# Reading the moving operand backwards in four projections, and shifting the weight tiles in steps of 64 bytes

## The chip, the cores and the metric

The kernel runs on one core of a Trainium2 chip. The metric is the device time of one execution in microseconds (us), the median of several runs; lower is better.

## What is computed

One layer of an autoregressive decoder on 256 tokens of width 2048, float32, and a final norm:

```python
h = rms_norm(x, ln1)
proj = h @ w_in                       # 2048 -> GDN q|k|v, beta, decay, z; MoBA q|k|v; gates a, b
qkv_a, beta_a, decay_a, z_a, qkv_b, gate_a, gate_b = split_columns(proj)
y_a = gated_deltanet(qkv_a, beta_a, decay_a, z_a, ...) @ w_branch_a      # 1024 -> 2048
y_b = moba_attention(rope(q_b), rope(k_b), v_b) @ w_branch_b             # 1024 -> 2048
merged = sigmoid(gate_a) * y_a + sigmoid(gate_b) * y_b
x = x + merged @ w_out                                                   # 2048 -> 2048
h = rms_norm(x, ln2)
u = causal_dwconv(h @ w_up, ffn_conv, ffn_conv_bias)                     # 2048 -> 2 x 5632
u_gate, u_val = split(u, 2)
x = x + (silu(u_gate) * u_val) @ w_down                                  # 5632 -> 2048
return rms_norm(x, final_norm)
```

## The kernel before

Activations lie transposed: 128 features of a block on the partitions, the 256 tokens along the free dimension. Every float32 operand of a projection is split into two parts that TensorE takes in one pass each, a high part (`wh`, `hh`) and the rest (`wl`, `hl`), and a product is the sum high x high + high x rest + rest x high. The two parts of an activation tile lie side by side (`hc`, `yc`, `mc`, `h2` are [128, blocks, 2, 256]), so that one matmul with `wh` as the stationary operand moves 512 columns (both parts of the activation) and one with `wl` moves 256 (the high part alone).

The stages follow each other: the GDN projections (PSUM tiles `ps_gdn`, `ps_z`), those of the attention (`ps_moba`, `ps_v`), the gates (`ps_gate`, 16 chunks), the two branch projections (`ps_br`, 8 times two chunks), the output projection (`ps_wo`, 8 chunks), the up projection (`ps_up`, 44 chunks) and the down projection (`pd`, 44 blocks of the hidden width, 24 matmuls each). Up to the fourth gate chunk the PSUM tiles are narrow and every matmul moves 256 columns; from then on they are wide. The GDN recurrence and the attention run as generators in the background, a step at a time between matmuls (`tick`, every 1700 units of matmul work).

`chunk` makes one PSUM tile from two weight tiles of 128 x 2048. `load_w` brings a weight tile by a DMA on SP's queue (`wraw`, four buffers), ACT copies it into `wh` (L118) and DVE subtracts to get `wl` (L115), both in pieces of 1024 columns; `wh` and `wl` have two buffers each. In `ps_v` and in the down projection the roles are exchanged: 512 columns of `wh` or `wl` move and 128 columns of an activation (`hc`; `ah`, `al`) are the weights. TensorE loads the weights of a matmul while the one before runs. In the compiled program the operand of each weight load begins at the last of its columns and steps by -1; the moving operand steps by +1.

All matmuls of `chunk` come from `main_mm` (L108), those of the down projection from `mmg` (L96). `yca` and `ycb` (L715) are the split branch outputs, `mc` the split merged branches, `h2` the split input of the up projection (L205, L206). In the recurrence, `X` (L514) is a copy of a unit matrix that is worked on in place and stored through a DRAM tile `dU` (L525) to be loaded as `U` (L527), and `Xa` (L512) comes through a DRAM tile `dA`. Which instruction stands where on an engine is set by a scheduler at build time; tile pools decide when a buffer can be written again.

Of the kernel before, what the change touches and what calls it, by code (L numbers as in the profile page):

```python
# [11 lines left out]
F32 = mybir.dt.float32  # L12
F32R = mybir.dt.float32r
# [6 lines left out]
P = 128  # L20
T = 256
D = 2048
KD = D // P
H = 8
KB = H
DFF = 5632
NF = DFF // P
EPS = 1e-6
EVERY = 1700
WIDE_AT = 4  # L30
ATT_SCALE = 128 ** -0.5
# [49 lines left out]
def layer_kernel(ctx: ExitStack, tc: tile.TileContext, xT, pos, cst, csel, ceye, vec, convw, ffw, bdv,  # L81
# [6 lines left out]
    wpool = wst.enter_context(tc.tile_pool(name="wpool", bufs=2))  # L88
# [4 lines left out]
    def mmg(ps, pairs, start=True, stop=True, **kw):  # L93
        n = len(pairs)
        for i, (a, b) in enumerate(pairs):
            pe.matmul(ps, a, b, start=(start and i == 0), stop=(stop and i == n - 1), **kw)  # L96
# [10 lines left out]
    def main_mm(ps, a, b, start, stop):  # L107
        pe.matmul(ps, a, b, start=start, stop=stop, skip_group_check=True)  # L108
        spent[0] += 215 if b.free_size() > T else 108
        if spent[0] >= EVERY:  # L110
            spent[0] = 0
# [5 lines left out]
    def split(hi, lo, src):  # L117
        act.copy(hi, src)  # L118
        return low(hi, lo, src)

    def three(ah, al, bh, bl):
        return [(ah, bh), (ah, bl), (al, bh)]
# [5 lines left out]
        sp.dma_start(raw[:, :n], src)  # L128
        return raw

    def load_w(src, n=2048, into=None, piece=1024, raw=None):
        raw = raw or fetch(src, n)
        wh, wl = into or [wpool.tile([P, 2048], F32R, name=t, tag=t) for t in ("wh", "wl")]
        for o in range(0, n, piece):
            lows.append(split(wh[:, o:o + piece], wl[:, o:o + piece], raw[:, o:o + piece]))
        return wh[:, :n], wl[:, :n]
# [8 lines left out]
    epst = keep.tile([P, 1], F32, name="epst")  # L145
    act.activation(epst, ones[:, 0:1], AF.Identity, scale=EPS)

# [26 lines left out]
            main_mm(ps, wh[:, k, :], x[:, k], k == 0, False)  # L174
            main_mm(ps[:, 0, :], wl[:, k, :], x[:, k, 0, :], False, k == kt - 1)

    def chunk(blocks, x, kt, name, raws=(None, None), piece=1024, steps=((0, 0, None), (1, 0, None))):
        ps = mmt("ps_" + name)
        ws = {}
        for j, k0, k1 in steps:  # L180
            if j not in ws:
                ws[j] = load_w(blocks[j], kt * P, raw=raws[j], piece=piece)
            block(ps[:, j], ws[j], x, kt, k0, k1)
        return ps

# [6 lines left out]
    def join(dst, ps, r):  # L192
        with tc.high_priority():
            join_(dst, ps, r)
# [26 lines left out]
    hp = hst.enter_context(tc.tile_pool(name="hp", bufs=1, side="right"))  # L221
    hc = hp.tile([P, KD, 2, T], F32R, name="hc", tag="hc")
# [4 lines left out]
    g = n1.enter_context(tc.tile_pool(name="n1", bufs=1, side="right"))  # L227
# [16 lines left out]
    for i in range(4):  # L244
        s = slice(4 * i, 4 * i + 4)
# [9 lines left out]
    raws = [fetch(w) for w in (w_gdn[2], w_gdn[3])]  # L255
# [38 lines left out]
    s = sdt("ps_bd")[:48, :T]  # L294
    mmg(s, [(wb2[:, k, :], x_[:, k, :]) for k in range(KD) for x_ in (hh, hl)])
    R1 = rstd([sq[0][:, 0, :], sq[0][:, 1, :]], fk, "R1")
    R1b = both(R1)
# [21 lines left out]
    m = m_st.enter_context(tc.tile_pool(name="m", bufs=2, reuse_waits="tile"))  # L319
    gdn_st = ExitStack()  # L320
    dr = gdn_st.enter_context(tc.tile_pool(name="dr", bufs=2, space=bass.MemoryType.DRAM))
    g = gdn_st.enter_context(tc.tile_pool(name="g", bufs=2, side="right", reuse_waits="tile"))
# [118 lines left out]
    def gdn(h0, kq, v):  # L441
# [9 lines left out]
        st = g.tile([P, 8, 4], F32, name="st")  # L451
        dve.tensor_scalar(st[:, 0, :], pq[:, :, 0], EPS, P * EPS, op0=ALU.add, op1=ALU.mult)

# [4 lines left out]
        for j in range(2):  # L458
            c = 8 + hs[j]
# [25 lines left out]
        act.activation(st[:, 2, :], st[:, 1, :], AF.Sqrt, bias=epst)  # L485
        dve.tensor_scalar(st[:, 3, :], st[:, 1, :], EPS, None, op0=ALU.add)
        dve.reciprocal(st[:, 3, :], st[:, 3, :])
# [20 lines left out]
        dA = dr.tile([4, P + 1, P], F32, name="dA")  # L508
        pool.dma_start(dA[0:2, :P].rearrange("j s c -> s j c"), aq0[:, :, 0, :P])
        pool.dma_start(dA[2:4, :P].rearrange("j s c -> s j c"), aq1[:, :, 0, :])  # L510
        Xa = g.tile([32, 16, 16], F32, name="Xa")
        pool.dma_start(Xa, diag(dA))  # L512
        X = g.tile([32, 16, 16], F32, name="X")
        pool.tensor_copy(X, eye)  # L514
        yield from wait(9)
        for i in range(1, 16):
            tm = g.tile([32, 16, 16], F32, name="tm", bufs=1)
            dve.tensor_tensor(tm[:, :i, :i], X[:, :i, :i], Xa[:, None, :i, i].to_broadcast([32, i, i]), op=ALU.mult)
            dve.tensor_reduce(X[:, :i, i], tm[:, :i, :i], axis=AX.X, op=ALU.add, negate=True)
            if i % 4 == 3:  # L520
                yield
        dU = dUs[h0 // 2 % 2]
        if h0 < 4:
            sp.dma_start(dU[:, :P].rearrange("p s c -> s p c"), zero[:, None, :].to_broadcast([P, 4, P]))
        pool.dma_start(diag(dU), X)  # L525
        U = g.tile([P, 4, P], F32, name="U0", tag="U", bufs=1)
# [54 lines left out]
        pool.tensor_tensor(so, ot, ot, op=ALU.mult)  # L581
        dve.tensor_reduce(st[:, 4, :], so, axis=AX.X, op=ALU.add)
        dve.scalar_tensor_tensor(st[:, 5, :], st[:, 4, :], 1.0 / P, st[:, 0, :], op0=ALU.mult, op1=ALU.add)
# [11 lines left out]
    def pair(w, i):  # L595
        return [w[2 * i], w[2 * i + 1]]

    for gr in range(4):
# [3 lines left out]
        for a, t in enumerate((kq[:, 1], kq[:, 0], v)):  # L602
            if gr == 0 and a < 2:
                ps = (ps_q0, ps_k0)[a]
            else:
                ps = chunk(pair(w_gdn, 4 * gr + a), hc, KD, "gdn")
# [58 lines left out]
    for gr in range(4):  # L665
        h0 = 2 * gr
        qk = []
        for a in range(2):
            ps = chunk(pair(w_moba, 2 * gr + a), hc, KD, "moba")
            t = m.tile([P, 2, T], F32, name=f"qk{a}")  # L670
            join(t, ps, R1b)
            qk.append(t)
        if gr % 2 == 0:
            ps = [mmt("ps_v").rearrange("p a b -> p (a b)") for _ in range(2)]
            for q_ in range(4):
                wh, wl = (r3(t, 512) for t in load_w(w_mv[2 * gr + q_]))
                for i in range(2):
                    s = slice(i * P, (i + 1) * P)
# [18 lines left out]
    gts = gp.tile([P, 16, 2, T], F32, name="gts")  # L697
    for c in range(16):
        if c == WIDE_AT:
            while bg:  # L700
                tick()
            wide[0] = True
            psum_pools(3, 2)
        join(gts[:, c], chunk(pair(w_gate, c), hc, KD, "gate"), R1b)
        act.activation(gts[:, c], gts[:, c], AF.Sigmoid)
    while bg:
        tick()
# [1 line left out]
    yp = y_st.enter_context(tc.tile_pool(name="yp", bufs=1, side="right", reuse_waits="tile"))  # L709
    yc = []  # L710
    for t, nm_ in ((ya, "a"), (yb, "b")):
        yc.append(yp.tile([P, H, 2, T], F32R, name="yc" + nm_))
        for i in range(4):
            s = slice(2 * i, 2 * i + 2)
            act.copy(yc[-1][:, s, 0, :], t[:, s])  # L715
            low(yc[-1][:, s, 0, :], yc[-1][:, s, 1, :], t[:, s], pool)
# [1 line left out]

    m_st = ExitStack()
    m = m_st.enter_context(tc.tile_pool(name="mp", bufs=1, reuse_waits="tile"))  # L720
    mc = m.tile([P, KD, 2, T], F32R, name="mc")
    for c in range(8):
        bts = [yp.tile([P, 2, T], F32, name="bt", bufs=3) for _ in range(2)]
        join(bts[0], chunk(pair(w_ba, c), yc[0], H, "br"), gts[:, c])
        ps = chunk(pair(w_bb, c), yc[1], H, "br")
# [15 lines left out]
    b = bp.enter_context(tc.tile_pool(name="b", bufs=2, reuse_waits="tile"))  # L741
    x1 = bkeep.tile([P, KD, T], F32, name="x1")
    sqa = b.tile([P, 2, T], F32, name="sqa", bufs=1)
    h2 = hp.tile([P, KD, 2, T], F32R, name="h2", tag="hc")
    for c in range(8):
        steps = ((0, 0, KD - 2), (1, 0, 8), (0, KD - 2, KD), (1, 8, KD))
        ps = chunk(pair(w_o, c), mc, KD, "wo", **({} if c else dict(piece=512, steps=steps)))
        if c % 2 == 0:
            s = slice(2 * c, 2 * c + 4)
# [18 lines left out]
    ak = bk.enter_context(tc.tile_pool(name="ak", bufs=1, side="right", reuse_waits="tile"))  # L768
    acts = ak.tile([P, NF, T], F32, name="acts")
    for c in range(NF):  # L770
        ps = chunk([w_up[c], w_up[NF + c]], h2, KD, "up")
        un = b.tile([P, 2, T], F32, name="unf")
        join(un, ps, R2b)
        t = b.tile([P, 2, T], F32, name="cvf")
        for j in range(2):
            w = ffv[:, j * NF + c, :]
            act.activation(t[:, j, :], un[:, j, :], AF.Identity, scale=w[:, 2:3], bias=w[:, 3:4])  # L777
            for d in (1, 2):
                dve.scalar_tensor_tensor(t[:, j, d:], un[:, j, :T - d], w[:, 2 - d:3 - d], t[:, j, d:],  # L779
                                         op0=ALU.mult, op1=ALU.add)  # L780
        sg = b.tile([P, T], F32, name="sg")
        act.activation(sg, t[:, 0, :], AF.Silu)  # L782
        pool.tensor_tensor(acts[:, c, :], sg, t[:, 1, :], op=ALU.mult)  # L783
# [8 lines left out]
    pd = [[ps_d.tile([P, 512], F32, name=f"pd{i}_{n}") for n in range(4)] for i in range(2)]  # L792
# [8 lines left out]
    wl = {}  # L801
    tail = hp.tile([P, 2, 2, 2048], F32R, name="tail", tag="hc")

    def down(i, n, k, stop=False):
        ah, al, wh, wl_ = wl[k]
        s, c = slice(i * P, (i + 1) * P), slice(n * 512, (n + 1) * 512)
        mmg(pd[i][n], three(ah[:, s], al[:, s], wh[:, c], wl_[:, c]), start=False, stop=stop,
            skip_group_check=True)

    for k in range(NF):  # L810
        last = k >= NF - LAST
        ab = LAST if last else 2
        ah = b.tile([P, T], F32R, name="ah", tag="ah" + "L" * last, bufs=ab)
        al = b.tile([P, T], F32R, name="al", tag="al" + "L" * last, bufs=ab)
        split(ah, al, acts[:, k, :])
        wh, wl_ = load_w(w_dn[k], into=[tail[:, t, k - NF + 2, :] for t in range(2)] if k >= NF - 2 else None)
        wl[k] = (ah, al, wh, wl_)
        if not last:
            for i, n in order:
                if k == 0:  # L820
                    residual(i, n)
                down(i, n, k)
# [88 lines left out]
```

## Time and profile before

| | |
|---|---|
| time, median of 3 runs | 1512.03 us (1511.71 to 1512.86) |
| span of the profiled execution, first to last instruction | 1506.8 us |
| what lies around the span, against the median | 5.2 us |
| TensorE matmul busy | 1489.5 us (99%) |
| weight loads busy | 1337.8 us (89%) |
| VectorE / ScalarE / GpSimd busy | 1021.3 / 753.5 / 169.7 us |
| granted TensorE clock, mean | 0.998 |

The profiled execution's own time beside its span is not recorded apart from the runs, so the median stands for it. Busy time of TensorE counts the time in which at least one matmul is in flight; matmuls overlap, so their pace is read from the starts. In the rows, a group is named by what it writes and what it reads (`ps_up<-h,wh`), with its line, engine and shape.

### The profile page before, as it was taken

The page shows a single profiled execution, that of the slowest core. Times are in us where ns is not written, and L with a number is a line of the kernel's source. Part 1 is how long each engine was busy: PE and PEld are TensorE (multiplying, and loading weights), DVE is VectorE, ACT ScalarE, POOL GpSimd, SP SyncE. Part 2 cuts the span into 40 slices and gives each one's busy share as a digit, 9 for nine tenths or more (in the row PEclk, how much of TensorE's full clock was granted, in tenths as well). Part 3 has the DMA queues.
Part 4 walks back from the last instruction along what each step waited for, and adds up shares of the span by engine and source line. Part 5 has one row for each costly group of instructions (what it writes and reads, how often), then busy time and mean ns, then how long its engine had stood idle before and what let it go on. Part 6 is the DMA issues. An engine that isn't in the chain of part 4 may idle for free.

```text
span 1506.8 us, 22467 instructions
## 1 busy us (share of the span) xinstructions
PE 1489.5 (99%) x9167; PEld 1337.8 (89%) x9167; DVE 1021.3 (68%) x1454; ACT 753.5 (50%) x1021; POOL 169.7 (11%) x133
## 2 busy tenths in 40 slices
PE   9999999999999999999999999999999999999997
PEld 8999999988998888888888888888888888888886
DVE  7988695886765555777667767677676776555554
ACT  5655463434474444454455555455554554444444
POOL 1001101042130000110101211211112110000000
PEclk9999999999999999999999999999999999999999
DMA  9444444444335553567555555555555555555552
GB/s 340 174 169 167 172 149 176 149 149 149 132 140 200 191 182 129 186 223 291 192 184 188 188 196 196 179 189 191 196 196 178 190 192 171 194 194 195 196 196 84
DMA packets 45639, 276.94 MB, mean 184 GB/s; under 512 B 5504, under 2 KB 6992, under 8 KB 15456
## 3 DMA queue, kind: packets, MB, share of 16 engines
q1 hardware_dynamic: 43712, 270.98, 51.1%
q0 software_dynamic: 960, 2.36, 0.5%
q10 hardware_dynamic: 864, 2.16, 0.4%
q8 instruction: 72, 1.18, 0.3%
q14 instruction: 31, 0.25, 0.0%
HBM read 271.68 MB, written 3.80 MB: 183 GB/s over the span
## 4 chain that ended last, share of the span: by engine, by line
PE 90%; DVE 5%; ACT 2%; DMA 1%; issue 1%; SPq 0%; POOL 0%; DVEq 0%; ACTq 0%
PE ps_up L108 32%; PE pd L96 16%; PE ps_gate L108 11%; PE ps_gdn L108 8%; PE ps_wo L108 6%; PE ps_br L108 5%; PE ps_moba L108 3%; PE ps_z L108 3%; PE ps_v L108 2%; DVE wl L115 2%; ACT wh L118 1%; DMA wraw<-in_w_gdn 1%; PE py L548 1%; PE g L96 0%; PE pu L554 0%
## 5 line engine op out<-in xcount | busy, mean ns | idle before, releaser
L115 DVE TENSOR_TENSOR wl<-wraw,wh 128x1024 fp32r<-128x1024 f32 (+1 forms) x500 | 607.0, 1247 | 264.1 <-ACT wh L118 263.7
L118 ACT CAST wh<-wraw 128x1024 fp32r<-128x1024 f32 (+1 forms) x500 | 497.7, 1040 | 383.1 <-PE ps_up L108 117.3
L108 PE MATMUL ps_up<-h,wh 128*128 128x512 f32 x1408 | 488.6, 390 | 0.0
L108 PE MATMUL ps_up<-h,wl 128*128 128x256 f32 x1408 | 397.0, 282 | 0.0
L108 PEld LDWEIGHTS ps_up<-h,wh 128*128 128x128 f32 x1408 | 264.4, 188 | 55.4
L108 PEld LDWEIGHTS ps_up<-h,wl 128*128 128x128 f32 x1408 | 266.1, 189 | 0.1
L108 PE MATMUL ps_gate<-hc,wh 128*128 128x512 f32 (+1 forms) x640 | 179.7, 347 | 0.0
L108 PE MATMUL ps_gate<-hc,wl 128*128 128x256 f32 x512 | 144.4, 282 | 0.2 <-DVE wl L115 0.2
L96 PE MATMUL pd<-wl,ah 128*128 128x512 f32 x336 | 130.8, 389 | 0.0
L96 PE MATMUL pd<-wh,al 128*128 128x512 f32 x336 | 130.8, 389 | 0.0
L783 POOL TENSOR_TENSOR acts<-sg,cvf 128x256 f32<-128x256 f32 x44 | 80.8, 1836 | 423.3 <-ACT sg L782 423.3
L108 PE MATMUL ps_gdn<-hc,wh 128*128 128x256 f32 x704 | 125.9, 281 | 0.0
L108 PEld LDWEIGHTS ps_gate<-hc,wh 128*128 128x128 f32 x640 | 111.4, 188 | 15.1
L108 PEld LDWEIGHTS ps_gdn<-hc,wh 128*128 128x128 f32 x704 | 107.5, 188 | 0.6 <-ACT wh L118 0.2
L777 ACT ACTIVATE cvf<-unf,ffv 128x256 f32<-128x256 f32 x88 | 48.2, 595 | 104.4 <-DVE unf L201 104.4
L108 PE MATMUL ps_gdn<-hc,wl 128*128 128x256 f32 x352 | 99.0, 281 | 0.8 <-DVE wl L115 0.8
L779 DVE SCALAR_TENSOR_TENSOR cvf<-unf,ffv,cvf 128x254 f32<-128x254 f32 (+1 forms) x176 | 77.3, 480 | 32.2 <-ACT cvf L777 31.8
L108 PEld LDWEIGHTS ps_gate<-hc,wl 128*128 128x128 f32 x512 | 96.7, 189 | 0.4 <-DVE wl L115 0.4
L108 PE MATMUL ps_moba<-hc,wh 128*128 128x256 f32 x512 | 93.4, 282 | 0.0
L96 PE MATMUL pd<-wh,ah 128*128 128x512 f32 x336 | 92.8, 391 | 0.0
L108 PE MATMUL ps_wo<-mc,wh 128*128 128x512 f32 x256 | 88.8, 391 | 0.0
L118 ACT CAST ah<-acts 128x256 fp32r<-128x256 f32 x44 | 17.9, 407 | 125.8 <-PE pd L96 116.1
(430 smaller groups left out, 2076.7 us busy)
## 6 DMA issues: line engine op xcount, KB each, us to landing
wraw<-in_w_up SPq DMA_DIRECT2D x88, 1024.0 KB, 4.8
wraw<-in_w_dn SPq DMA_DIRECT2D x44, 1024.0 KB, 4.8
wraw<-in_w_gate SPq DMA_DIRECT2D x32, 1024.0 KB, 4.8
wraw<-in_w_gdn SPq DMA_DIRECT2D x30, 1024.0 KB, 4.9
wraw<-in_w_moba SPq DMA_DIRECT2D x16, 1024.0 KB, 4.8
wraw<-in_w_o SPq DMA_DIRECT2D x16, 1024.0 KB, 4.8
wraw<-in_w_mv SPq DMA_DIRECT2D x8, 1024.0 KB, 4.9
wraw<-in_w_ba SPq DMA_DIRECT2D x16, 512.0 KB, 3.4
```

The source lines that it names most:

```text
L96: pe.matmul(ps, a, b, start=(start and i == 0), stop=(stop and i == n - 1), **kw)
L108: pe.matmul(ps, a, b, start=start, stop=stop, skip_group_check=True)
L115: return (eng or dve).tensor_tensor(lo, src, hi.bitcast(F32), op=ALU.subtract)
L118: act.copy(hi, src)
L548: pe.matmul(py[:, p], ats[p], Tm[:, p], start=True, stop=True)
L777: act.activation(t[:, j, :], un[:, j, :], AF.Identity, scale=w[:, 2:3], bias=w[:, 3:4])
L779: dve.scalar_tensor_tensor(t[:, j, d:], un[:, j, :T - d], w[:, 2 - d:3 - d], t[:, j, d:], op0=ALU.mult, op1=ALU.add)
L783: pool.tensor_tensor(acts[:, c, :], sg, t[:, 1, :], op=ALU.mult)
```

## The change

The four activation tiles `yca`, `ycb`, `mc` and `h2` are used through views that are reversed in the part and token axes: what is written to them goes down in memory, and a matmul that moves 512 or 256 columns of them steps by -1 through memory from the end. In the down projection each row of `w_dn` is reversed in blocks of 512 on its way into the input array, and the moving read of `wh` and `wl` is reversed to match. The products are the same, column by column. The gate, GDN and attention projections keep their forward reads.

The weight tiles get 128 columns (512 bytes) of room, and a tile begins `at` columns into it: 16 columns (64 bytes) per step, over eight places in the gate and up projections (c % 8), nine in the down projection (k // 5); the others stay at 0. `Xa` and `X` have one buffer instead of two.

```diff
+PAD = 128
...
-    def load_w(src, n=2048, into=None, piece=1024, raw=None):
+    def load_w(src, n=2048, into=None, piece=1024, raw=None, at=0):
         raw = raw or fetch(src, n)
-        wh, wl = into or [wpool.tile([P, 2048], F32R, name=t, tag=t) for t in ("wh", "wl")]
+        wh, wl = into or [wpool.tile([P, 2048 + PAD], F32R, name=t, tag=t)[:, at:at + 2048] for t in ("wh", "wl")]
...
-    def chunk(blocks, x, kt, name, raws=(None, None), piece=1024, steps=((0, 0, None), (1, 0, None))):
+    def chunk(blocks, x, kt, name, raws=(None, None), piece=1024, steps=((0, 0, None), (1, 0, None)),
+              at=0):
...
-                ws[j] = load_w(blocks[j], kt * P, raw=raws[j], piece=piece)
+                ws[j] = load_w(blocks[j], kt * P, raw=raws[j], piece=piece, at=at)
...
-        Xa = g.tile([32, 16, 16], F32, name="Xa")
+        Xa = g.tile([32, 16, 16], F32, name="Xa", bufs=1)
...
-        X = g.tile([32, 16, 16], F32, name="X")
+        X = g.tile([32, 16, 16], F32, name="X", bufs=1)
...
-        join(gts[:, c], chunk(pair(w_gate, c), hc, KD, "gate"), R1b)
+        join(gts[:, c], chunk(pair(w_gate, c), hc, KD, "gate", at=16 * (c % 8)), R1b)
...
-        yc.append(yp.tile([P, H, 2, T], F32R, name="yc" + nm_))
+        yc.append(yp.tile([P, H, 2, T], F32R, name="yc" + nm_)[:, :, ::-1, ::-1])
...
-    mc = m.tile([P, KD, 2, T], F32R, name="mc")
+    mc = m.tile([P, KD, 2, T], F32R, name="mc")[:, :, ::-1, ::-1]
...
-    h2 = hp.tile([P, KD, 2, T], F32R, name="h2", tag="hc")
+    h2 = hp.tile([P, KD, 2, T], F32R, name="h2", tag="hc")[:, :, ::-1, ::-1]
...
-        ps = chunk([w_up[c], w_up[NF + c]], h2, KD, "up")
+        ps = chunk([w_up[c], w_up[NF + c]], h2, KD, "up", at=16 * (c % 8))
...
-        mmg(pd[i][n], three(ah[:, s], al[:, s], wh[:, c], wl_[:, c]), start=False, stop=stop,
+        mmg(pd[i][n], three(ah[:, s], al[:, s], wh[:, c][:, ::-1], wl_[:, c][:, ::-1]), start=False, stop=stop,
...
-        wh, wl_ = load_w(w_dn[k], into=[... tail ...] if k >= NF - 2 else None)
+        wh, wl_ = load_w(w_dn[k], into=[... tail ...] if k >= NF - 2 else None, at=16 * (k // 5))
...
-        "w_dn": np.asarray(w_down)[0].reshape(NF, P, D),
+        "w_dn": np.asarray(w_down)[0].reshape(NF, P, 4, 512)[..., ::-1].reshape(NF, P, D),
```

The order of instructions is the same on TensorE, VectorE, ScalarE and SP. On GpSimd one row moves. Before, in the third group of heads of the recurrence, GpSimd's rows are these (`sqq` squares k, `dA`, `Xa`, `dU`, `U` are the DMAs named above, `Y` is cleared for the next step); the copy of X for the fourth group has long been done, since X has a second buffer:

```order
L445 TENSOR_TENSOR sqq<-kq 128x512
L509 DMA dA<-aq_2218 128x2x128
L510 DMA dA<-aq_2219 128x2x128
L512 DMA Xa<-dA 32x16x16
L544 MEMSET Y 128x8x32
L544 MEMSET Y 128x4x64
L525 DMA dU_395<-X 32x16x16
L544 MEMSET Y 128x16x16
L527 DMA U_2640<-dU_395 128x4x128
```

In the changed kernel, whose lines are one or two further down, the same place reads:

```order
L447 TENSOR_TENSOR sqq<-kq 128x512
L511 DMA dA<-aq_2218 128x2x128
L512 DMA dA<-aq_2219 128x2x128
L514 DMA Xa<-dA 32x16x16
L546 MEMSET Y 128x8x32
L546 MEMSET Y 128x4x64
L527 DMA dU_395<-X 32x16x16
L516 COPY X<-eye 32x256
L546 MEMSET Y 128x16x16
L529 DMA U_2640<-dU_395 128x4x128
```

The copy of X for the fourth group now stands behind the store of X by this group, and has to wait until that store has landed.

More of the change, by code (lines that the diff above doesn't have):

```diff
@@ L815, in layer_kernel @@
         split(ah, al, acts[:, k, :])
-        wh, wl_ = load_w(w_dn[k], into=[tail[:, t, k - NF + 2, :] for t in range(2)] if k >= NF - 2 else None)
+        wh, wl_ = load_w(w_dn[k], into=[tail[:, t, k - NF + 2, :] for t in range(2)] if k >= NF - 2 else None, at=16 * (k // 5))
         wl[k] = (ah, al, wh, wl_)
```

## The prediction

> **What bounds the kernel now.** I read the page's busy table first, then the chain that ended last in order of time, then a table by stage, then the groups with shapes kept apart.
>
> ```profile
> span 1506.8 us, 22467 instructions
> PE 1489.5 (99%) x9167; PEld 1337.8 (89%) x9167; DVE 1021.3 (68%) x1454; ACT 753.5 (50%) x1021; POOL 169.7 (11%) x133
> PE 90%; DVE 5%; ACT 2%; DMA 1%; issue 1%; SPq 0%; POOL 0%; DVEq 0%; ACTq 0%
> ```
>
> TensorE is busy for 99% of the span and is 90% of the chain. Times are added to the profiled execution: its span is 1506.8 us, and the median of the runs, 1512.03, lies 5.2 us above it, which I take as unchanged. Busy is no measure of pace, since a matmul overlaps the next; the chain gives pace, as a piece's length over its count:
>
> ```profile
> 32.93 3.63 PE ps_bd L96 x32
> 60.47 16.33 PE ps_gdn L108 x140
> 340.29 8.39 PE ps_v L108 x36
> 677.05 88.75 PE ps_wo L108 x512
> 772.39 483.26 PE ps_up L108 x2788
> 1264.02 235.03 PE pd L96 x1035
> ```
>
> So one matmul every 113.4 ns in ps_bd, 116.6 in ps_gdn, 233.1 in ps_v, 173.3 in ps_wo, 173.3 in ps_up (a 512-column and a 256-column one in turn: 346.7 a pair) and 227.1 in pd. The stages from the output projection on are one unbroken run of matmuls.
>
> What a matmul would take with nothing in its way is the slope between two shapes, and the weight load's pace is found the same way:
>
> ```profile
> L108 PE MATMUL ps_up<-h,wh 128*128 128x512 f32 x1408 | 488.6, 390 | 0.0
> L108 PE MATMUL ps_up<-h,wl 128*128 128x256 f32 x1408 | 397.0, 282 | 0.0
> L108 PEld LDWEIGHTS ps_up<-h,wl 128*128 128x128 f32 x1408 | 266.1, 189 | 0.1
> L96 PEld LDWEIGHTS ps_bd<-hc,wb 128*48 128x48 f32 x32 | 3.6, 121 | 0.0
> ```
>
> (390 - 282)/256 = 0.42 ns per moved column: 216 ns for 512, 108 for 256. (189 - 121)/80 = 0.85 ns per weight column: 109 ns for 128, half the pace of the moving read. The excess over the moving time is then 11.1 ns in pd (227.1 - 216), 22.7 a pair in ps_up and ps_wo (346.7 - 324), 8.6 in ps_gdn, 17.1 in ps_v, and 5.4 in ps_bd, whose load has 48 columns instead of 128. Fewer loaded columns, less excess: the next load, which runs beside the moving read, slows it. ps_v and pd do the same (512 moved columns beside a 128-column load) and differ by 6.0 ns, so the cost depends on how the two reads lie to each other, and that is what the change touches: in the compiled program a weight load's operand begins at the tile's last column and steps by -1, the moving read stepped by +1, and now both step by -1.
>
> **The change part by part.**
>
> *Reversed moving reads.* 2816 matmuls of ps_up, 512 of ps_wo, 512 of ps_br and 1056 of pd keep their number, order and size; only the excess can change. No row shows a load and a moving read in the same direction, so I bound it.
> - Gain: the whole excess goes. 1408 x 22.7 = 32.0 us in ps_up, 256 x 22.7 = 5.8 in ps_wo, the same at most in ps_br, 1056 x 11.1 = 11.7 in pd: 55 us.
> - Loss: the moving read catches up with the slower load and is held to its pace until the load ends. If held from the start, 109 - 54 = 55 ns per matmul; with starting distances spread evenly half of that, 27, in place of the 11 of now: 16 ns x (2816 + 1056) = 62 us.
> - Between them lies the nearest row, ps_v's 17.1 ns. At that price ps_up pays 1408 x (34.2 - 22.7) = 16.2 us, ps_wo 2.9, ps_br 2.9, pd 1056 x 6.0 = 6.3: 28 us.
>
> Going the same way, the faster read closes on the load at the difference of their paces and not at the sum, so an overlap of places lasts three times as long though it comes less often; I hold that for a loss sooner than a gain. Since the weight tiles begin at eight or nine places in ps_up and pd, I let half of the chunks fall in ps_v's state and half stay as they are: 14 us.
>
> *Tiles 64 bytes apart.* The offset alone, with forward reads, comes in the gate stage: 384 pairs and 384 narrow matmuls over eight places. In the program of before all weight tiles begin at one place modulo 512 bytes and the moving tiles of ps_up and ps_wo at two others, yet both stages have 173.3 ns. I take nothing; the ends are ps_v's price for the pairs, +384 x 11.5 = 4 us, and their whole excess, -384 x 22.7 = 9 us.
>
> *Writes with a negative step.* ACT and DVE write yca, ycb, mc and h2 downwards, POOL subtracts into yca and ycb so.
>
> ```profile
> L715 ACT CAST ycb<-yb x4: 620/622/623, 440.5 to 442.0; 128x512 fp32r<-128x512 f32 x4
> L115 POOL TENSOR_TENSOR ycb<-yb,ycb x4: 2270/2276/2279, 444.1 to 450.8; 128x512 fp32r<-128x512 f32 x4
> L118 ACT CAST mc<-gts x9: 407/622/625, 600.1 to 682.5; 128x512 fp32r<-128x512 f32 x7, 128x256 fp32r<-128x256 f32 x2
> L206 DVE SCALAR_TENSOR_TENSOR h<-x,vc,h x16: 473/476/1523, 692.8 to 769.8; 128x256 fp32r<-128x256 f32 x16
> 584.08 13.76 PE ps_br L108 x79
> ```
>
> POOL's last ycb ends by 454 us and the branch projection begins at 584, so even at double time it is covered by 130 us of gate matmuls. The mc and h2 writes are spread through stages where TensorE has work; only the last h2 pieces (769.8) are close to their reader, some 2 us if those instructions took twice as long. Taken at 0, bounds 0 and +2.
>
> *One buffer for X and Xa.* Only POOL's row order changes: group 3's copy of X now stands behind group 2's store of X. Behind it on POOL wait the clear of Y and the load of U.
>
> ```profile
> 233.29 0.65 POOL L525 DMA_DIRECT2D dU<-X  x1 [7.62 <-DVE X L519]
> 238.17 0.31 POOL L544 MEMSET Y<- 128x256 f32 x1 [4.22 <-PE pu L554]
> L514 POOL COPY X<-eye x4: 410/696/938, 24.8 to 167.7; 32x256 f32<-32x256 f32 x4
> L525 POOL DMA_DIRECT2D dU<-X x4: 653/654/677, 123.0 to 324.4; - x4
> DMA to landing us min/median/max: 2.4/3.7/6.1
> ```
>
> The clear of Y stood idle for 4.22 us after the store, for TensorE. Landing and copy take 2.4 + 0.7 at best (covered), 6.1 + 0.9 at worst, 2.8 us late, and only this once; Xa's load waits for the group before, which by then has ended. Taken at 0, bound +3.
>
> *What gives way in ps_br.* There TensorE is paced in part by the making of weights, and a slower matmul uses up that wait first:
>
> ```profile
> 583.00:677.00 94.00, 91.69 (x520) 79.49 (x519) 71.32 (x73) 46.74 (x60) 9.01 (x7) 1.00 0.57 191
> 766.00:1255.00 489.00, 489.00 (x2821) 433.48 (x2820) 340.14 (x443) 259.01 (x359) 80.04 (x43) 1.00 0.54 189
> 598.95 2.23 DVE wl L115
> ```
>
> Columns: window, length, then busy time of PE, PEld, DVE, ACT, POOL. TensorE idles 2.3 us of 94 in ps_br, so up to 2.3 us of its loss would vanish, and a gain there would end in the wait for wl. In ps_up DVE is busy for 340 of 489 us and ACT for 259, so neither takes over if TensorE becomes faster.
>
> Sum: 1506.8 + 14 + 0 + 0 + 0 + 5.2 = 1526 us. On its own this case reaches from 1515 (just slower) to 1540 (all of ps_v's price).
>
> **The rivals.**
>
> *The reads keep out of each other's way (faster).* Two reads that go the same way and don't start at the same place need not meet at all during a load. If half of the excess of ps_up, ps_wo and pd goes (ps_br's is partly given back to wl): (32.0 + 5.8 + 11.7)/2 = 25 us, 1487 us; all of it, 1462. For it speaks ps_bd's 5.4 ns: the excess is tied to the load and not to the matmul. Against it, the moving read is twice as fast, so it does not keep its distance, and excess is between 8.6 and 17.1 ns in every 128-column row, never near zero. It decides the sign as soon as the excess of a ps_up pair falls below 22.7.
>
> *Direction is of no account (same).* Then each pace stays: 1512. For it, ps_wo and ps_up begin their moving tiles at different places and have the same 173.3 ns; against it, ps_v's 17.1 beside pd's 11.1. [...]
>
> *Held to the load's pace (much slower).* The bound above, +62 us: 1574. It comes true if the reads share a place in most chunks, and would show as ps_up pairs near 379 ns. A moving read that is itself slow at a negative step would look alike, but would not vary from chunk to chunk; against it, only the sign changes and the data stay adjacent. [...]
>
> **How the numbers follow.** Forecast (up to +28 us) 0.33; held to the pace or a slow step 0.14; faster 0.31; no change 0.22. About 0.2%, 3 us, is what a measurement of this kernel can tell from no change. Faster 0.31, same 0.22, slower 0.47. The range goes down to 1472 (four fifths of the faster case's excess in ps_up, ps_wo and pd gone: 0.8 x 49.5 = 40 us) and up to 1575, the held case; outside are the last part of the faster case and the dearer tail, together under 0.2.
>
> **What would show it.** In the chain after: a ps_up piece whose length over count is above 173.3 ns and differs between chunks with the place of the weight tile; pd above 227.1; ps_gate as before; ps_gdn and ps_moba, which are not touched, at 116.6 to 118. Right: ps_up near 176 ((346.7 + 5.75)/2), pd near 230. [...] If ps_br starts late after the gate stage, the negative-step writes cost what I left out. I am wrong in the sign if reads of the same direction settle into a distance that they then keep.

## The result, and the profile after

The changed kernel takes 1527.52 us (median of 4 runs, 1526.4 to 1529.31) against 1511.87 before (1508.53 to 1512.86): ratio 1.0116, 95% interval 1.0099 to 1.0132. The forecast was 1526.0. In every run that has both numbers 1.7 to 1.9 us lie around the span (here 1526.4 against 1524.6 in the profiled execution). So the 5.2 us given for the kernel before is not what lies around a span: its profiled execution, by this estimate about 1508.6 us, was faster than the median. In the chain in order of time the same stages stand, longer. Two rows of before were not shown yet, the gate's and one of six alike in the branch projections:

```profile
445.31 138.77 PE ps_gate L108 x814
...
601.23 8.27 PE ps_br L108 x46
```

The span and the chain of the changed kernel (start, length, engine, tile, line, instructions):

```profile
span 1524.6 us, 22466 instructions
445.49 139.84 PE ps_gate L109 x814
585.33 14.03 PE ps_br L109 x79
678.81 90.45 PE ps_wo L109 x512
775.91 490.96 PE ps_up L109 x2788
1275.31 241.54 PE pd L97 x1035
```

From one piece's start to the next, with the rows of the prediction: up to the gate +0.2 us, gate +1.1, branch projections +0.5 (93.48 against 92.97), output projection with what follows it +1.8, up projection +7.8, down projection to the end +6.5. That is 17.8 us, the whole difference of the two spans. Per matmul: ps_up 176.1 ns (173.3 before), pd 233.4 (227.1), ps_wo 176.7 (173.3). Nothing on this chain waits anew: the copy of X did wait 4.36 us for the store to land, and the clear of Y behind it came 1.2 us later than before, but neither is on the chain. The wide matmul of the up projection itself is longer, while its weight load keeps its 188 to 189 ns (groups of the tile, forms apart: shortest, mean, longest ns, first and last start):

```profile
L109 PE MATMUL ps_up<-h,wh x1408: 395/397/587, 769.8 to 1266.4; 128*128 128x512 f32 x176
L109 PEld LDWEIGHTS ps_up<-h,wl x1408: 187/188/191, 770.0 to 1266.4; 128*128 128x128 f32 x176
```

397 ns against 390. Within the up projection two paces alternate with the place of the weight tile. The chain cut to the inside of one chunk at offset 64 bytes and of one at 0 gives a pair 10.88 / 31 = 351.0 ns and 10.96 / 31 = 353.5, where before every chunk had 346.7:

```profile
872.39 10.88 PE ps_up L109 x62
861.09 10.96 PE ps_up L109 x62
```

### The profile page after: what moved, and what is told of

It reads as the page before. It is cut to its first block, busy times and chain, and to the rows that moved or that the text cites. A ratio compares the mean times of both kernels' runs of the same rounds, so it can differ in the third digit from the quotient of the medians.

```text
span 1524.6 us, 22466 instructions
## 1 busy us (share of the span) xinstructions
PE 1508.1 (99%) x9167; PEld 1336.5 (88%) x9167; DVE 1020.7 (67%) x1454; ACT 753.0 (49%) x1021; POOL 169.2 (11%) x133
## 3 DMA queue, kind: packets, MB, share of 16 engines
q8 instruction: 72, 1.18, 0.3%
## 4 chain that ended last, share of the span: by engine, by line
PE 91%; DVE 5%; ACT 1%; DMA 1%; issue 1%; SPq 0%; DVEq 0%; POOLq 0%; ACTq 0%
PE ps_up L109 33%; PE pd L97 16%; PE ps_gate L109 11%; PE ps_gdn L109 8%; PE ps_wo L109 6%; PE ps_br L109 5%; PE ps_moba L109 3%; PE ps_z L109 3%; PE ps_v L109 2%; DVE wl L116 2%; ACT wh L119 1%; DMA wraw<-in_w_gdn 1%; PE py L550 0%; PE g L97 0%; PE pu L556 0%
## 5 line engine op out<-in xcount | busy, mean ns | idle before, releaser
L109 PE MATMUL ps_up<-h,wh 128*128 128x512 f32 x1408 | 496.3, 397 | 0.0
```

## The experiments

A pair is a wide (512 moved columns) and a narrow (256) matmul in turn. "By the starts" means: worked out from the start times of successive matmuls in the trace. Tiles' places are those of the compiled programs; a distance is the first byte of the moving tile less that of the weight tile, modulo 256 bytes. In the kernel before it is 0 in pd and ps_wo, 32 in ps_gdn, ps_gate, ps_br and ps_up, and 224 in ps_v. In the experiments on the up projection with fewer loaded or moved columns part of the layer's product is left out, and reversed chunks there give their columns in reverse; all but one of the edited kernels are built on the changed kernel with its reversal taken out where the text says forward, so they keep the room in the weight tiles and the single buffers of X and Xa.

### Offsets alone

```diff
-        yc.append(yp.tile(...)[:, :, ::-1, ::-1])     (likewise mc, h2, and w_dn with its two reads)
+        yc.append(yp.tile(...))
```

> Undoes the reversal and keeps the offsets of the gate, up and down projections. Meeting theory (a weight load and a moving read get in each other's way according to how they lie): the gate's forward readings carry over, so a pair in the up projection takes 346.6, 352.9, 346.8 and 350.2 ns at offsets 0, 64, 128 and 192 bytes, 349.1 in the mean, +3.5 us; the gate +1.1 us; the down projection moves off 226.7 ns at some offsets, 0 to +4 us; 1516 to 1520 us. Step theory (the negative step alone costs, offsets do not): up and down stay at 346.7 and 226.7, 1513 us with the gate's +1.

1517.22 us against 1508.96, ratio 1.0060 (1.0045 to 1.0075). The chain, then the inside of up chunks at offset 0, 64 and 192 bytes, then pd's pieces at 64, 128 and 192:

```profile
773.52 486.70 PE ps_up L118 x2788
1268.59 238.67 PE pd L106 x1035
858.04 10.75 PE ps_up L118 x62
869.13 10.95 PE ps_up L118 x62
891.52 10.85 PE ps_up L118 x62
1292.02 26.32 PE pd L106 x115
1319.51 26.72 PE pd L106 x115
1347.40 26.84 PE pd L106 x115
```

A pair takes 346.8, 353.2 and 350.0 ns by offset (346.8 at 128 by the starts), and pd 228.9, 232.3 and 233.4 ns (226.7 at 0); from 256 bytes on the list repeats. So a forward read has a price that goes with the place of the weight tile, and no place that was tried is cheaper than 0: the offsets cost 3.4 us in the up projection, 3.6 in pd and, as in the changed kernel, 1.1 in the gate. That is what the meeting theory expected; the step theory, by which offsets are free, falls.

### Reversal alone

```diff
-        ps = chunk([w_up[c], w_up[NF + c]], h2, KD, "up", at=16 * (c % 8))     (likewise gate and w_dn)
+        ps = chunk([w_up[c], w_up[NF + c]], h2, KD, "up", at=0)
```

> Keeps the reversal in all four projections, all weight tiles at offset 0. Both theories: a pair in the up projection at 353.2 ns (the changed kernel's reading at offset 0), +9.2 us; down 233.3 ns, +7.0; output projection 353.3, +1.7; branch projections +0.3: about 1530 us. If offsets are what costs and the reversal is free, 1512.

1525.3 us against 1508.96, ratio 1.0104 (1.0087 to 1.0121).

```profile
778.55 489.45 PE ps_up L118 x2788
1276.43 241.53 PE pd L106 x1035
```

The up projection pays 6.2 us (9.2 expected: a pair took 351.1 ns, not 353.2), pd 6.5, the output projection 1.7 (90.46). The two halves of the change do not add: 0.60% and 1.04% against 1.16% together. In pd the reversal alone costs as much as the whole change, and in the up projection 6.2 and 3.4 become 7.7. So the two costs overlap; in pd they are the same cost.

### Fewer loaded columns, and reversal by blocks

```diff
+            main_mm(ps[:n], wh[:, k, :n], x[:, k], k == 0, False)          n = 128, 64 or 32 weight columns
+            main_mm(ps[:n, 0, :], wl[:, k, :n], x[:, k, 0, :], False, k == kt - 1)
```

> All weight tiles at offset 0. In the up projection five chunks each: forward and reversed moving reads beside weight loads of 128 columns, of 64, of 32, and with the 512-column matmul split into two of 256; outputs of the left-out columns and of reversed chunks are not the reference's. In the down projection ten blocks each: forward, all reversed, blocks of 16 columns taken in descending order but read ascending inside, and the other way round. Meeting theory: the cost of reversal shrinks with the loaded columns, from 6.6 ns per pair at 128 to about 3.3 at 64 and 1.7 at 32, and so does the forward excess of 22.7; the descending blocks cost like the full reversal. Step theory: reversal costs 6.6 ns per pair at every width, and in the down projection only the ways with a step of -1 inside the block cost 6.6.

Up projection: 128 columns reversed, 32 forward, 32 reversed; then pd with blocks of 16 columns in descending order (ascending inside), and with ascending blocks that descend inside:

```profile
835.00 44.87 PE ps_up L119 x254
1003.14 44.36 PE ps_up L119 x255
1058.86 44.59 PE ps_up L119 x254
1372.92 50.17 PE pd L107 x215
1428.92 57.06 PE pd L107 x215
```

A reversed pair takes 353.3 ns with 128 loaded columns and 351.1 with 32; a forward one 346.7 with 128 (44.03 us for 254) and 347.2 with 32 (by the starts, once settled). The reversal alone had 351.1 beside 128 columns, so the 2.2 ns between the reversed pairs can't be put down to the width of the load, and a forward pair gains nothing from a shorter one; 64 columns gave 351.1 and 346.7 (by the starts). My reading of ps_bd ("fewer loaded columns, less excess") falls. With the wide matmul split in two, a row of narrow ones took 116.6 ns forward and 117.8 reversed (by the starts). Nor does the negative step have one price: descending blocks with ascending columns cost 233.3 ns, as much as a full reversal (233.3), and ascending blocks with descending columns 266.7 (all three by the starts). The meeting theory expected the first of these figures, and neither theory the last.

### Fewer moved columns

```diff
+            for w_ in (wh, wl):
+                main_mm(p[:m, :n], w_[:, k, :m], xk[:, 512 - n:][:, ::-1] if rev else xk[:, :n], ...)
```

> Offset 0. In the up projection, four chunks each, all matmuls move the same number of columns: 512 beside loads of 128 columns, forward and reversed; then 512, 384, 256 and 128 beside loads of 32 columns, forward and reversed; at last 384 beside 128, forward. What the layer computes there is left out. Start theory: the excess over 0.417 ns per column is a fixed sum per matmul, 13.3 ns forward and 20 reversed at each width, whatever the load. If the moving read is slower per column: excess in proportion to the columns, 3.3 ns forward at 128. If times fall on a grid of 6.67 ns: every reading in the mean is a multiple of it.

512 columns beside a 128-column load, forward and reversed; 512 and 256 forward beside a 32-column load:

```profile
783.41 45.97 PE ps_up L119 x197
845.01 45.97 PE ps_up L119 x197
906.58 45.89 PE ps_up L119 x197
1116.20 3.28 PE ps_up L119 x28
```

233.4 and 233.4; 232.9 and 117.1 ns. In a stream of wide matmuls alone at distance 32 the reversal costs nothing, because the forward read is just as slow. And beside a load of 32 columns the excess over the slope goes roughly with the columns moved (17 ns over 216 for 512, 9 over 108 for 256; 384 columns took 177.0 by the starts, 15 over 162), where the start theory had one fixed sum. At 256 columns it is no less than ps_gdn's 8.6 ns beside 128.

### Places 16 bytes apart, forward, with one tile or both moved, and reversed

```diff
-        ..., at=16 * (k // 5))
+        ..., at=4 * (k // 2 % 16))                        (likewise gate, up and output projection)
```

> Forward reads; weight tiles begin at 16 places 16 bytes apart in the gate and up projections, 16 places in the down projection, 8 places 32 bytes apart in the output projection. Meeting theory: a pair's time varies smoothly with the place between 346.6 and 353 ns, with a period of 256 bytes as the changed kernel's gate stage has it, and may go below 346.6 at places not tried; mean near 349. Step theory: no view on it. If the 64-byte grid is the unit, the four places inside one 64-byte step read alike.

pd's pieces at 64 and 208 bytes:

```profile
1313.22 9.85 PE pd L106 x43
1413.60 10.09 PE pd L106 x43
```

229.1 and 234.7 ns; over all 16 places 226.7 to 234.7, the least at 0 and at 240, and no up chunk below 346.5 (by the starts). No place is better than that of the kernel before. For pairs the place is not all: at 64 bytes they took 346.8 here, 353.2 with the offsets alone, and 353.6 through eleven chunks in a row in the next run. Here the chunk before lay at 48 bytes, there at 0 or 64; that pairs keep something from the chunk before is argued from this, not tried.

```diff
+        ah = b.tile([P, T + 64], F32R, name="ah", ...)[:, sh:sh + T]     (al likewise; sh = the offset of wh and wl)
```

> Forward reads. In the down projection the moving tile is shifted in 16-byte steps as in f1_fine_offsets, and the tiles that are loaded as weights (ah, al) by the same amount, so that the two keep their place to each other; in the up projection the weight tile stays at one of 0, 64, 128, 192 bytes for eleven chunks in a row. Start theory (each matmul's first reads and the next load's first reads get in each other's way, by their place to each other): 226.7 ns at every shift in the down projection, where f1_fine_offsets had 226.6 to 234.8. Own theory (the cost is the moving read's alone, by its start and direction): the same list as in f1_fine_offsets. In the up projection a pair is constant through each run of eleven, 346.6, 353.3, 346.6 and 350 ns by e1_forward_offsets; if history counts, 64 bytes can also read 346.6 as f1_fine_offsets had it.

With both tiles of pd moved by 32 and by 80 bytes (1514.48 us against 1512.2):

```profile
1286.04 9.77 PE pd L106 x43
1318.93 9.89 PE pd L106 x43
```

227.2 and 230.0 ns, where the moving tile alone had brought 233.3 and 231.0. Moved together, all even steps of 16 bytes kept 226.7 to 226.9 once settled and all odd ones had 230.0 to 230.1 (by the starts): what counts is for the most part where the two tiles lie to each other, and at odd steps their own place costs 3.4 ns more.

```diff
-        at=16 * (c % 8)), at=16 * (k // 5))
+        at=4 * (c % 16)), at=4 * (k // 2 % 16))          (reads stay reversed)
```

> Reversed reads, weight tiles at 16 places 16 bytes apart in the up and down projections. Start theory: direction shifts which places are good, so some of the 16 places bring the reversed down projection to 226.7 ns and a pair in the up projection to 346.6, as forward reads have it. Own theory: reversed reads stay at 233.3 and 351 to 353 at every place.

```profile
775.01 491.47 PE ps_up L118 x2788
1274.92 241.86 PE pd L106 x1035
```

Reversed, no place is cheap: 351.1 to 353.5 ns per pair (one chunk 356.5), pd 233.3 to 233.5 at fourteen places and 236.6 at two (by the starts). That is the own theory's answer; the start theory, by which some places would be as cheap as forward, falls.

### The weight tile alone moved

```diff
+        ah = b.tile([P, T + 64], F32R, ...)[:, sh:sh + T]                 sh = 4 * (k // 2 % 16), wh and wl stay
+        ps = chunk(..., "up", part=PART[c // 4], at=PART[c // 4][2])      512 columns in both products
```

> Forward reads. Down projection: only the weight tiles move, in steps of 16 bytes every two chunks (modulo 256), the moving tile stays. Up projection: both products of a step stream 512 columns (the w_lo product gets 512 instead of 256, and with 64 or 32 weight columns the other rows are left out, so this part of the computation is changed), in groups of four chunks: 128 loaded columns with the weight tile at 192 modulo 256 bytes (moving tile at 224); 128 columns at 224; 64 there; 32 there; 32 columns 128 bytes further; 128 at 224 with the moving read reversed; 128 columns at 288 forward, and reversed; 352; 416; 192 again. Theory (the distance of the moving tile from the loaded tile modulo 256 bytes counts, and a reversed read is dear at every distance): at 192 both theories 233.3 ns per matmul, as measured; at 224, distance 0, 226.7 forward with 128 columns and 233.3 reversed; with 64 and 32 columns there 226.7 if the tile's first byte counts, more if the last loaded column counts. Down projection 226.7 at distance 0, up to 234.8 elsewhere, the piece about 240 us. Rival (each tile's own place counts): moving weights alone does nothing in the down projection, 226.7 throughout, and all forward groups of the up projection stay at 233.3. Whole kernel some 90 us above before, for the longer streams: 1605.

1697.87 us in one run; I had put the longer streams at some 90 us, a slip: 1408 x (231 - 118) ns is 159, and 88 first matmuls stand beside them, 20 more. Up projection at distance 0 with 128, 64 and 32 loaded columns; reversed at 0 with 128; forward at distance 128 and 64; then pd at 64 (weights moved by 192):

```profile
829.72 59.61 PE ps_up L120 x263
889.56 60.41 PE ps_up L120 x263
950.20 60.83 PE ps_up L120 x263
1072.25 61.41 PE ps_up L120 x263
1257.21 61.12 PE ps_up L120 x263
1318.56 60.20 PE ps_up L120 x263
1578.70 9.84 PE pd L108 x43
```

226.7, 229.7, 231.3; 233.5; 232.4, 228.9; 228.8 ns. Two stages with different tiles agree: distance 0, 64 and 128 give 226.7, 228.9 and 232.4 here, and 226.7, 228.9 and 232.3 in pd when its moving tile was moved. The 16 places of pd in this run, where only the loaded tiles moved, set beside those of the fine offsets, where only the moving tile did, show how far this goes (by the starts): at distances that are multiples of 32 bytes the two agree within 0.4 ns, but for 128 (233.4 here, 232.4 there); at odd multiples of 16 they differ by up to 4.9 (226.7 here, 231.6 there at distance 16, once settled). So in a row of wide matmuls the distance sets most of the pace, whichever tile is moved, and each tile's own place some of it. With 32 loaded columns the wide matmul at distance 0 is slower by 4.6 ns, not faster, and 231.0 with the weights moved 128 bytes further: neither of the two answers that I had for it, first byte or last loaded column, fits. Reversed, the cheap place is gone (233.5 ns at distance 0 against 226.7).

### Tiles aligned in the kernel before

```diff
-    hc = hp.tile([P, KD, 2, T], F32R, name="hc", tag="hc")        (likewise h2 and tail)
+    hc = the same tile, 32 bytes lower                             (yca and ycb, which lie next to them, move too)
```

> The kernel before with the tiles hc, h2 and tail, which the moving reads of V, the gate, the up projection and the last matmuls stream, begun 32 bytes lower (192 modulo 256 bytes, where the weight tiles begin). Nothing else changes, all reads are forward. Theory (distance modulo 256 bytes): ps_v goes from 233.2 to 226.7 ns, 192 matmuls x 6.5 ns = 1.25 us less, and the last matmuls after the steady part of pd from about 233 to 226.7, 0.3 us less; ps_gate and ps_up stay at 346.7 ns per pair, which is the least that any distance gave. Whole kernel 1510.4 against 1512, ratio 0.999. Rival (own place counts): no change, 1512.

1527.59 us against 1509.73, ratio 1.0118 (1.0100 to 1.0137): as slow as the change, with no read reversed.

```profile
61.96 16.80 PE ps_gdn L108 x140
345.00 8.21 PE ps_v L108 x36
450.91 141.46 PE ps_gate L108 x814
781.12 492.54 PE ps_up L108 x2788
```

V's wide matmuls fall from 233.1 to 228.1 ns and the last ones after pd to 226.7 (by the starts), the way that was expected (226.7 for both). But the narrow ones of ps_gdn go from 116.6 to 120.0, and the pairs of gate and up projection from 346.7 to 353.3. My expectation that pairs stay at 346.7 was wrong: the rule holds in rows of wide matmuls, and narrow ones take less at another distance, 32.

### Wide ones first

```diff
+        for k in range(kt): main_mm(ps, wh[:, k, :], x[:, k], k == 0, False)
+        for k in range(kt): main_mm(ps[:, 0, :], wl[:, k, :], x[:, k, 0, :], False, k == kt - 1)
+        up: at=PART[c // 4][1:]                                    places of the high and the low part apart
```

> The kernel before with only the up projection changed, all reads forward (moving tile at 224 modulo 256 bytes), in groups of four chunks: the weight tile of the high part, or that of the low part, or both, moved by 32 bytes (from 192 to 224, distance 0), and the 16 wide matmuls of a half done either in turn with the 16 narrow ones, as before, or all wide ones first. Theory A (a matmul's time depends on the distance of its moving tile from the weight tile that is loaded beside it; wide: 226.7 ns at distance 0, 233.3 at distance 32 bytes; narrow: 116.6 at 32, 119.9 at 0): wide first gives 349.9 per pair with both at 192, 343.3 with the high part moved, 353.2 with the low part moved, 346.6 with both. In turn, the load beside a wide read is that of the low part: 346.7 with both at 192, 343.3 with the low part moved, 350 to 353 with the high part moved; with both moved 346.7 or 353.3, as two runs had it. Theory B (its own loaded weights count): in turn, low and high part change places; wide first, the same as A. Rival C (distance is not what counts in streams of two widths): in turn, all four give 346.7 or 353.3 and wide first is not below 346.7. Whole kernel 1509 to 1513.

In turn, with the high part's tile at distance 0 and the low part's at 32; then wide ones first with both at 32, with the high part alone at 0, and with the low part alone at 0:

```profile
857.26 45.09 PE ps_up L120 x255
947.31 44.10 PE ps_up L120 x252
992.11 43.51 PE ps_up L120 x252
1036.31 44.42 PE ps_up L120 x252
```

Wide first gives pairs of 350.0, 345.3 and 352.5 ns (expected 349.9, 343.3, 353.2), and 348.1 with both at 0 (by the starts; expected 346.6). In turn, three of the four placings have 346.7, and that with the high part at distance 0 has 353.3. Theory B had 343.3 for that one and falls. Theory A, the tile loaded beside the read, has it right but expected 343.3 where the low part is moved, and 346.7 came. For pairs in turn rival C's bare "346.7 or 353.3" is all that holds: with both parts at distance 0 they took 346.7 here and 353.3 in the kernel with the aligned tiles. Why narrow reads take less at 32 bytes (116.6 ns, 120.0 at 0) and wide ones at 0 (226.7, 233.3 at 32) stays open.

### A version that uses it

```diff
+            for j in range(2):                                      (both halves' wide matmuls, then the narrow ones)
+                for k in range(kt): main_mm(ps[:, j], ws[j][0][:, k, :], x[:, k], k == 0, False)
+            for j in range(2):
+                for k in range(kt): main_mm(ps[:, j, 0, :], ws[j][1][:, k, :], x[:, k, 0, :], False, k == kt - 1)
+    high part moved by 32 bytes (gate, branch, up), low part by 224 (output), V's moving tiles by 32;
+    the last chunk of the branch projections and the first of the output projection stay in turn
```

> A version of the kernel before, all reads forward. In the branch, gate (its twelve wide chunks), output and up projections all wide matmuls of a chunk come first (both halves, 32 in a row, 16 in the branch projections), then its narrow ones; the high part's weight tile is moved so that the wide reads are at distance 0 from it modulo 256 bytes, the low part's so that the narrow ones are at 32. V's moving tiles are moved to distance 0 from hc. Theory (the distance of a moving tile from the tile loaded beside it, in a row of one width): wide 226.7 ns after some 33 ns of settling per row, narrow 116.6: 344.3 per pair against 346.7: 1408 x 2.4 = 3.4 us in the up projection, 384 x 2.4 = 0.9 in the gate, 224 x 2.4 = 0.5 in the output projection, 192 x 6.5 = 1.25 us in V; the branch projections, where weights arrive late in part, 0 to 1 us more. 6 us in all: 1506 against 1512, ratio 0.996. Rival (the other order costs elsewhere what it wins: chunks end with both halves at once and the next stage starts later, or buffers of the low part come free too late): the pairs reach 344 to 345 and the whole time stays at 1511 to 1513.

1502.25 us against 1509.78, ratio 0.9953 (0.9939 to 0.9967): 0.5% faster than the kernel before.

```profile
445.31 137.86 PE ps_gate L118 x814
583.17 81.98 PE ps_br L118 x472
672.10 86.40 PE ps_wo L118 x496
766.99 481.51 PE ps_up L118 x2801
```

The pairs of the up projection take 344.4 ns (227.8 + 116.6 by the starts), as expected. Of the 3.2 us that this gives only 1.0 reaches the end: with wide ones first the last piece of h2 is asked for after 15 wide matmuls (3.4 us) instead of 15 pairs (5.2 us), so the first chunk waits longer; that cause is argued, not tried. Another 0.7 us go at the passage to pd, 9.08 us instead of 8.37, where the chain now waits for wl. V's gain does not reach the end: the gate begins at 445.31 us as before. The largest gain is one that I had put at 0 to 1 us: from the start of the branch projections to that of the output projection 88.93 us instead of 92.97. Their pieces of 8.27 us, each ended by the wait for wl, have become one unbroken run of 472 matmuls, since a chunk now asks for the low part only after its wide matmuls. That the sum came as expected, 6.5 us between the spans against 6, is luck: its terms were off both ways.

> The version with all wide matmuls of a chunk first, in the same order, but with every weight tile at its old place (192 modulo 256 bytes; wide reads of the gate, branch and up projections at distance 32, those of the output projection and its narrow ones at 0). Theory (placing gave the pace, the order gave the branch projections their time): up 233.3 + 116.6 = 349.9 per pair, 1408 x 3.3 = 4.6 us slower than before, gate 384 x 3.3 = 1.3 slower, output projection about 347.8 per pair, 0.3 slower, V as before, branch projections still 3 to 4 us shorter than before: 1513 against 1510, ratio 1.002, and 10 to 11 us slower than the version with the tiles placed. Rival (the order alone gave the gain): ratio 0.995 as there.

The diff is the one above without the moves of its tiles. 1517.35 us against 1510.65, ratio 1.0042 (1.0027 to 1.0057).

```profile
449.20 140.03 PE ps_gate L118 x814
589.23 83.08 PE ps_br L118 x472
679.25 87.00 PE ps_wo L118 x496
774.75 490.20 PE ps_up L118 x2801
```

The order alone keeps the gain in the branch projections (90.02 us) and loses 1.3 us in the gate, as expected, and in the up projection 7.7 from its start to pd's instead of 4.6, part of it the longer wait of the first chunk, part of it that the narrow matmuls of every second chunk took 117.9 ns (by the starts). Of the 10.0 us between this span (1516.8) and that of before 3.9 lie ahead of the gate, in stages that this version leaves as they were; why is not known. From the gate on, it takes 12.6 us more than the version with the tiles placed: at one and the same order of instructions the placing is worth about 0.8%.

## Why the prediction was right, and where it was not

- **Sign and size.** +14 us forecast, +15.6 between the medians, +17.8 between the spans. That the forecast lies within 1.5 us of the measured time is in part luck: the stages cost 3.8 us more than the sum had, and the 5.2 us that it added to the span were 3.4 too many, since the runs have some 1.8 there.
- **The up projection** (8 us, "near 176") came out at 7.8 us and 176.1 ns, but not in the way told: I let half of the chunks stay as they were and half pay ps_v's 11.5 ns per pair. Every chunk pays, 4.4 or 6.7 ns per pair.
- **The down projection** (half of 6.3 us, "near 230") pays the whole: 233.4 ns at all nine places, 6.5 us. The step that failed is "half of the chunks in ps_v's state": no place spared a reversed read, though nine places here and sixteen in the fine steps were tried. The price of ps_v's row itself, 6.0 ns per wide matmul, was nearly right for pd (6.3); for pairs, 11.5 was too much.
- **Output and branch projections** (1.45 us each at half price): 1.8 and 0.5. In the branch projections TensorE idled 1.6 us instead of 2.3, so 0.7 us of the loss went into the wait for wl, as forecast.
- **Offsets alone** were taken at 0 (bounds -9 and +4). In the gate they cost 1.1, within the bounds; with forward reads throughout they cost 8, most of which the reversal hides, since a place that is already lost can't be lost again. That ps_wo and ps_up, at two places, have the same 173.3 ns was no sign that places are free: for pairs both happen to be at the lowest pace.
- **Writes with a negative step and the shared buffer** at 0: the branch projection starts where the gate ends (445.49 + 139.84 = 585.33), and ahead of the gate 0.2 us were added.
- **The cause was wrong.** I held the next load for what slows a moving read, and read that from ps_bd's 5.4 ns beside 48 columns. Load widths of 128 and 32 gave 233.4 and 232.9 ns at distance 32, and at distance 0 the shorter load made the matmul slower (226.7 to 231.3). The runs show in its place that a row of forward wide matmuls takes 226.7 to 234.7 ns by where its two tiles lie, and a row of reversed ones 233.3 at most places and never less. The kernel before had pd (226.7) and its pairs (346.7) at the lowest pace that any place gave. Reversal loses it everywhere, offsets in three of four places of 64 bytes for pd and in two of four for pairs. Why ps_bd's row (113.4 ns) is faster than the other rows of narrow matmuls shown stays open: 32 loaded columns at distance 32 gave 117.1, and its own place was not varied.
- **The rivals.** "Faster" is out: no reversed place is below 351.1 or 233.3 ns. "Held to the load's pace" is out: pairs near 379 never came; its +62 us counted ps_up and pd alone, and the 1024 matmuls of ps_wo and ps_br at the same 16 ns would have been 16 us more. "Direction of no account" holds only where the forward read is slow already, in rows of wide matmuls at distance 32 (233.4 both ways) and 192 (233.3 and 233.5). Beside a load of 128 columns a wide matmul took hardly longer than beside one of 32 (233.4 and 232.9 ns at distance 32), but where the loaded tile lies does count: moving the weight tile alone by 32 bytes took a wide matmul from 233.3 to 226.7 ns.
- **The step of -1.** I held against a slow step that the data stay adjacent; no run shows that this helps. In pd that step took 233.3 ns against 226.7, and 266.7 with short runs turned round; but forward reads took up to 234.7 at other places.

What makes a moving read faster at some distances (226.7 ns at 0 against 233.3 at 32 for wide ones in a row) and never when it is reversed (233.3 or more) is not settled: no run shows the cause. For pairs something besides the distance counts, since at one distance they took 346.7 ns in one run and 353.3 in another. The direction of the load was the same in all runs and wasn't varied.

## What to carry to other kernels

When successive matmuls run without a gap and still take longer than the slope between two shapes gives for their columns (here 226.7 to 234.7 ns where it gave 216), compare their pace, start to start, between stages of equal shape: a difference can be a matter of where the tiles lie. Here a shift of 32 bytes cost up to 1.2% of the kernel (1527.59 us against 1509.73). Before moving or reversing operands, note at which place the tuned kernel stands, since one that is already at its best place can only lose by a move. Matmuls of two widths took least at different places here (512 columns 226.7 ns at distance 0, 256 columns 116.6 at 32); done in rows of one width, each can have its own (344.4 ns per pair in the up projection instead of 346.7), and the operand that is made last (wl) is asked for later.

## What was not expected of the hardware

- One and the same matmul of 512 columns beside a 128-column load took 226.7 to 234.7 ns, read forward, by the places of its two tiles modulo 256 bytes, tried in steps of 16 bytes.
- Reversed, the same matmul took 233.3 to 233.5 ns at fourteen of sixteen places and 236.6 at two.
- Lowering the moving tiles by 32 bytes cost 1.18%, as much as the whole change.
- Narrow matmuls (256 columns) took 116.6 ns at distance 32 and 120.0 at 0; wide ones in rows took 233.3 and 226.7.
- A read of ascending blocks of 16 columns that descend inside took 266.7 ns, the dearest of all.
